# Input weights of the mixing block: split during retention and read back from DRAM, its convolution taps rearranged

## The chip, the cores and the metric

One core of one Trainium2 chip runs the whole program. The metric is the device time of one execution in microseconds (us), as the median over runs. Five engines work side by side, each through its own list of instructions in a fixed order: TensorE (PE, matmul; its weight loads are PEld), VectorE (DVE), ScalarE (ACT), GpSimd (POOL) and SyncE (SP, which here only issues DMAs). DMAs move data between DRAM and the on-chip memory (SBUF).

## The reference, cut to what matters

Two blocks of a network on 1024 tokens of width 1024. The first has four branches (a to d, sparse, banded, stick-breaking attention and retention), each gated and merged by products with the normalised input `h`; the second is the mixing block with an MLP behind it.

```python
def hybrid_layer(x, c, ...):
    h = rms_norm(x, norm_g) * (1.0 + scale) + shift
    ... = jnp.split(h @ w_in, IN_OFFSETS, axis=-1)
    for i, (y, z) in enumerate(branches):          # d, retention, comes first in the kernel
        yi = y.reshape(B, S, BRANCH_W) * jax.nn.silu(z)
        term = jax.nn.sigmoid(h @ w_merge[i]) * (yi @ w_br[i])
        merged = term if merged is None else merged + term
    return x + gate * (merged @ w_out)

def second_block(x, p, ...):
        z = rms_norm_2(h, g_mix_pre[i]) @ w_in[i]
        conf_ab, q, k, v, f_logit, sc_h, sc_b, sc_c, pool_v = jnp.split(z, SPLIT_IDX, axis=-1)
        y_conf = conformer_conv(conf_ab, ...)      # a * sigmoid(b), 31 taps per channel, norm, silu, product
        y_att = forgetting_attention(q, k, v, f_logit + b_forget[i])      # 4 heads, softmax
        y_sc = sc_b * causal_depthwise_conv(sc_c * sc_h, w_sc[i])         # 3 taps
        y_pool = multiscale_pool(pool_v, ...)
        mix = jnp.concatenate([y_conf, y_att, y_sc, y_pool], axis=-1) @ w_out[i]
```

Retention, with chunks of 128 tokens, n = 0 to 7: scores of the chunk with a decay mask, times v, plus `q` times a state `R` that is handed from chunk to chunk; then each head is normalised.

## The kernel before, in words

All float32 operands of the large products are split into two parts, hi (the value rounded by a copy) and lo (the rest), and a product is three matmuls, hi by hi, hi by lo, lo by hi (`mm3`, L229 to L231). A product of 512 columns over a depth of 1024 is 24 matmuls. Weights are loaded by `load_w` (L187 to L205) in slabs of 128x1024 (512 KB): a raw tile `wr` by a DMA on SP's queue (L194), a hi tile `wh` by `copy` (L147 on ScalarE, L149 on VectorE) and a lo tile `wl` by `sub_lo` (L155 on POOL, L157 on VectorE). All three come from one set of nine buffers, tag "w"; a slab can be loaded only when a buffer is free. Wider tiles (activations, accumulators) come from 31 "blk" buffers.

A scheduler reads the program in the order written, gives each instruction its place on its engine by priorities and its own estimate of the time, and so fixes the lists. `stream(name, priority)` ranks what is issued inside it.

**Branch d** (L665 to L755) runs retention. Per chunk: scores (L700) into PSUM tiles `s`, mask on VectorE (L702), the product with `R` (L711) and with v (L714) into `o`, the state's update (L724 on TensorE, L731 on VectorE), statistics and normalisation (L737 to L744), transposes (L276) back. Behind a chunk, `FD` (L25, used at L751) may put other work: 'g' is `pre` (L635 to L652), a group of four merge products `h @ w_merge` whose tanh (L647) is stored to DRAM by SP (L649); 'b' is the sum for the gate of the layer. Its value is {0: 'g', 1: 'b', 6: 'g'}. After the loop, `y.gate` makes the product with `z` and silu. PSUM tiles of such products are called `mm`.

**Mixing** (L1286 to L1600). Its input weights `w_in_2` are loaded and split by `load_w` group by group: conformer a and b (`conf_group`, two channel halves m), q and k of the first two heads (`qk_group`), v with the forget logits (`tok_group`), then short convolution, pooling, the second q and k. The conformer's 31 taps (`tap`, L1329 to L1334) are VectorE instructions over 512 columns: two channel halves m by two token halves, 124 in all. `conv_steps` (L242) hands them out in turn; the string `WORK` (L25, loop at L1610) sets what follows: 's0' and 's1' the short convolution, 'A' and 'B' tiles of the attention over the first and second two heads, 'p' pooling, 't' and 'u' the rest of the taps, 'c' the rest of the conformer. After each A tile CS=4 tap steps are handed out. `softmax_pair` (L828 to L866) scales the probabilities of two heads through `copy` (L150 on VectorE) on the engine that `NORM2` names. `k_tiles` makes hi and lo tiles of k, with the unused 64 rows of each lo tile cleared on POOL (L770); `scores` (L797, L799) multiplies.

## Time and profile before

| | us |
|---|---|
| median of 3 runs | 2337.06 |
| lowest and highest | 2331.92, 2338.48 |
| the profiled execution | 2339.66 |
| its span on the core | 2337.8 |

The profile is of one execution, at a mean granted TensorE clock of 0.988. Its times count from the span's start. Busy shares are PE 96%, DVE 65%, ACT 41%, POOL 21%. Retention runs from about 78 to 228 us, mixing from about 1195 to 1560. Matmuls overlap in the records: their ends are modelled, so the distance of two starts tells the rate, and the busy time somewhat more than that.

### The profile page before, as it was taken

The numbers are of one execution on the slowest core, as the hardware profiler recorded it, in microseconds if no ns is written. First come the engines' busy times: TensorE is split into PE (matmuls) and PEld (weight loads), VectorE is DVE, ScalarE is ACT, GpSimd is POOL, SyncE is SP. The second block draws the span as 40 slices with busy tenths as digits, with TensorE's granted clock in tenths as the row PEclk, the third lists the DMA queues.
The fourth block names the chain that finished last, engine by engine and source line by source line (L and its number), as shares of the span: only waits on it lengthen the run. The fifth ranks groups of instructions, "written<-read, shape, count | busy, mean of one in ns | idle before, by whom it ended". The sixth has DMA issues, their size and how long they took to land.

```text
span 2337.8 us, 30294 instructions
## 1 busy us (share of the span) xinstructions
PE 2239.1 (96%) x11004; PEld 1854.8 (79%) x11004; DVE 1519.8 (65%) x2952; ACT 963.0 (41%) x1937; POOL 491.1 (21%) x411
## 2 busy tenths in 40 slices
PE   8999999999988999999998998999999999999898
PEld 6788888888877778877887876777888878888787
DVE  7634456665677865634479777756666776677773
ACT  6211344444545544422322344534544453344442
POOL 4222100010265622234320000012143430000021
PEclk9999999999999999999999999999999999999999
DMA  9421221122132343224221210156556595534222
GB/s 326 156 92 62 59 68 55 46 86 68 41 102 79 109 132 94 83 80 153 90 73 36 64 59 28 56 179 205 169 182 191 194 360 193 173 108 157 94 75 90
DMA packets 202783, 272.72 MB, mean 117 GB/s; under 512 B 17086, under 2 KB 126214, under 8 KB 202634
## 3 DMA queue, kind: packets, MB, share of 16 engines
q1 hardware_dynamic: 194240, 257.95, 34.1%
q10 hardware_dynamic: 8394, 12.84, 1.7%
q8 instruction: 87, 1.43, 0.3%
q14 instruction: 62, 0.51, 0.1%
...
## 4 chain that ended last, share of the span: by engine, by line
PE 46%; DVE 6%; DMA 2%; ACT 1%; issue 1%; POOL 0%; SPq 0%; DVEq 0%; POOLq 0%; ACTq 0%
PE mm L230 6%; PE mm L231 6%; PE mm L229 6%; DVE blk L1334 2%; PE s L1674 2%; PE s L1676 2%; PE s L1675 2%; PE t L276 1%; PE t L2014 1%; PE t L2015 1%; PE t L2016 1%; PE s L2015 1%; PE mm L2015 1%; PE s L2016 1%; PE mm L2016 1%; PE t L1674 1%
## 5 line engine op out<-in xcount | busy, mean ns | idle before, releaser
L229 PE MATMUL mm<-blk,wh 128*128 128x512 f32 x1264 | 505.1, 400 | 16.3 <-DVE tz L1149 7.0
L230 PE MATMUL mm<-blk,wh 128*128 128x512 f32 x1264 | 501.1, 396 | 0.9 <-DVE blk L157 0.9
L231 PE MATMUL mm<-blk,wl 128*128 128x512 f32 x1264 | 499.9, 396 | 1.9 <-POOL wl L155 1.5
L229 PEld LDWEIGHTS mm<-blk,wh 128*128 128x128 f32 x1264 | 238.6, 189 | 68.5 <-DVE tz L1149 9.8
L231 PEld LDWEIGHTS mm<-blk,wl 128*128 128x128 f32 x1264 | 238.6, 189 | 52.0 <-POOL wl L155 1.9
L230 PEld LDWEIGHTS mm<-blk,wh 128*128 128x128 f32 x1264 | 238.7, 189 | 47.5 <-DVE blk L157 1.3
L155 POOL TENSOR_TENSOR wl<-wr,wh 128x1024 fp32r<-128x1024 f32 (+1 forms) x50 | 122.6, 2453 | 479.7 <-ACT wh L147 281.3
L229 PE MATMUL mm<-wh,blk 128*128 128x512 f32 (+3 forms) x544 | 197.3, 364 | 6.2 <-DVE wh L149 1.8
L231 PE MATMUL mm<-wh,blk 128*128 128x512 f32 (+3 forms) x544 | 194.9, 360 | 1.0 <-DVE blk L157 1.0
L157 DVE SCALAR_TENSOR_TENSOR wh<-blk,wh 128x1024 fp32r<-128x1024 f32 x116 | 138.5, 1222 | 72.0 <-issue 56.4
L147 ACT ACTIVATE wh<-blk 128x1024 fp32r<-128x1024 f32 x116 | 116.9, 1053 | 163.1 <-PE s L2015 77.2
L230 PE MATMUL mm<-wl,blk 128*128 128x512 f32 (+3 forms) x480 | 171.1, 357 | 9.5 <-DVE wl L157 9.1
L147 ACT ACTIVATE blk<-mm 64x512 fp32r<-64x512 f32 (+3 forms) x138 | 77.9, 570 | 172.6 <-PE mm L231 112.6
L147 ACT ACTIVATE PT<-t 128x512 fp32r<-128x512 f32 (+3 forms) x224 | 96.0, 460 | 117.4 <-PE o L816 65.0
L157 DVE SCALAR_TENSOR_TENSOR PT<-t,PT 128x512 fp32r<-128x512 f32 (+3 forms) x224 | 110.9, 515 | 38.0 <-ACT PT L147 37.2
L147 ACT ACTIVATE wh<-wr 128x1024 fp32r<-128x1024 f32 (+2 forms) x91 | 93.7, 1031 | 99.4 <-DMA wr<-in_w_in_dram 22.5
L309 POOL TENSOR_TENSOR sm<-sm,mhalf 128x1 f32<-128x1 f32 x64 | 38.0, 597 | 444.3 <-DVE sm L308 428.6
L229 PEld LDWEIGHTS mm<-wh,blk 128*128 128x128 f32 x544 | 104.1, 192 | 24.5 <-DVE wh L149 2.6
L231 PEld LDWEIGHTS mm<-wh,blk 128*128 128x128 f32 x544 | 104.1, 192 | 16.9 <-DVE blk L157 1.8
L230 PEld LDWEIGHTS mm<-wl,blk 128*128 128x128 f32 x480 | 92.3, 192 | 24.2 <-DVE wl L157 11.3
L157 DVE SCALAR_TENSOR_TENSOR wl<-wr,wh 128x1024 fp32r<-128x1024 f32 (+2 forms) x69 | 88.2, 1279 | 30.8 <-PE mm L230 14.0
L1150 POOL TENSOR_TENSOR acc<-tz,acc 128x512 f32<-128x512 f32 x48 | 68.8, 1436 | 132.0 <-DVE tz L1149 91.4
...
## 6 DMA issues: line engine op xcount, KB each, us to landing
...
```

The source lines that it names most:

```text
L147: return ac.activation(dst, src, AF.Copy, scale=1.0 if scale is None else scale)
L155: po.tensor_tensor(lo, x, hi.bitcast(F32), op=ALU.subtract)
L157: ve.scalar_tensor_tensor(out=lo, in0=x, scalar=scale, in1=hi.bitcast(F32), op0=ALU.mult, op1=ALU.subtract)
L229: pe.matmul(dst, sh, mh, start=(i == 0), stop=False)
L230: pe.matmul(dst, sh, ml, start=False, stop=False)
L231: last = pe.matmul(dst, sl, mh, start=False, stop=(i == n - 1))
L1150: po.tensor_tensor(acc[:], t[:], acc[:], op=ALU.add)
L1334: ve.scalar_tensor_tensor(out=acc[:, c:c1], in0=u[:, c - l:c1 - l], scalar=w, in1=acc[:, c:c1], op0=ALU.mult, op1=ALU.add)
L1674: pe.matmul(dst, wh, xh, start=first and k == 0, stop=False, skip_group_check=True)
L1675: pe.matmul(dst, wh, xl, start=False, stop=False, skip_group_check=True)
L2015: pe.matmul(d, sh[:, c, ts_], tl[:, c, :], start=False, stop=False)
L2016: last = pe.matmul(d, sl[:, c, ts_], th[:, c, :], start=False, stop=stop)
```

## The change

1. `w2_split` splits all of `w_in_2` in 20 steps: 16 slabs of 128x1024 and 4 of 128x520. A step loads the raw slab (SP, two DMAs where it holds two groups of columns), makes hi on ScalarE and lo on VectorE, and stores both to DRAM (SP). `FD` calls three steps behind each of the chunks 0 to 6 of retention.
2. In mixing `load_w2` reads hi and lo by DMAs on POOL's queue; no split is left there.
3. The taps: channel half m=0 takes taps 0 to 15 by token halves, 16 to 30 over whole rows of 1024; m=1 takes all 31 over whole rows. `conv_steps` ranks them behind by TAPL=1000, and finishes one series before the next. 't' in `WORK` now stands for all that is left of them, 'u' is gone.
4. One of the two scalings of `softmax_pair` in the mixing's attention is on ScalarE (`NORM2='av'`).
5. `k_tiles` keeps one lo tile for two heads; nothing is cleared, and the lo matmul contracts 64 rows.
6. `short_conv` multiplies by `sc_b` straight from PSUM, in two halves, without a copy of it. Two casts (`identR`, `causR`) are issued earlier.

```diff
-_T = dict(..., FD={0: 'g', 1: 'b', 6: 'g'}, ..., NORM='v', NORM2='v', CS=4, CSB=8, ..., WORK='s0 A A A A A A A A p s1 q t c B c B c B c B c 0a 1a P w 5 4 6 7 g 2 3a e u c B e c B c e B c c e B 1b 0b 3b', ...)
+_T = dict(..., FD={0: 'gw', 1: 'bw', 2: 'w', 3: 'w', 4: 'w', 5: 'w', 6: 'gw'}, ..., NORM='v', NORM2='av', TAPL=1000, CS=4, CSB=8, ..., WORK='s0 A A A A A A A A p s1 q t c B c B c B c B c 0a 1a P w 5 4 6 7 g 2 3a e c B e c B c e B c c e B 1b 0b 3b', ...)
...
     def conv_steps(n):
-        for _ in range(n):
-            if convs:
-                half, steps_ = convs.pop(0)
-                if next(steps_, "end") != "end":
-                    convs.insert(sum(h == half for h, _ in convs), (half, steps_))
+        with stream("taps", tc.tile_snap_priority() + _T["TAPL"]):
+            for _ in range(n):
+                if convs and next(convs[0], "end") == "end":
+                    convs.pop(0)
...
+    w2_cols, w2_d = {}, {}
+    for m in range(2):
+        w2_cols["conf", m] = ([m * P, 256 + m * P], P, 4)
+    w2_cols["qk", 0] = ([512, 768], P, 4)
+    w2_cols["v", 0] = ([1024], 260, 2)
+    w2_cols["qk", 1] = ([512 + P, 768 + P], P, 4)
+    for m in range(2):
+        w2_cols["sc", m] = ([1284 + m * P, 1796 + m * P], P, 4)
+        w2_cols["sb", m] = ([1540 + m * P], P, 8)
+    w2_cols["pool", 0] = ([2052], 256, 4)
+
+    def w2_split():
+        for key, (cs_, n, per) in w2_cols.items():
+            N = n * len(cs_)
+            for b in range(KC // per):
+                raw = main.tile([P, per, N], F32, name=nm("wr"), tag="w", bufs=NW)
+                for i, c0 in enumerate(cs_):
+                    sy.dma_start(raw[:, :, i * n:(i + 1) * n], w_in2[:, b * per:(b + 1) * per, c0:c0 + n])
+                hi, lo = [main.tile([P, per, N], F32R, name=nm("wh"), tag="w", bufs=NW) for _ in range(2)]
+                copy(hi[:], raw[:], "a")
+                sub_lo(lo[:], raw[:], hi[:])
+                for j, t in enumerate((hi, lo)):
+                    d = dram.tile([P, per, N], F32R, name=nm("w2"), tag=nm("w2"), bufs=1)
+                    sy.dma_start(d[:].bitcast(F32), t[:].bitcast(F32))
+                    w2_d[key, b, j] = d
+                yield
+
+    def w2_ahead():
+        for _ in range(3):
+            next(w2_steps, None)
+
+    def load_w2(*key):
...
+        for b in range(KC // per):
+            for j, p_ in enumerate((w.h, w.l)):
+                p_[b] = main.tile([P, per, n * len(cs_)], F32R, name=nm("wh"), tag="w", bufs=NW)
+                po.dma_start(p_[b][:], w2_d[key, b, j][:])
...
             for c in _T["FD"].get(n, ""):
-                dict(g=pre, p=lambda: proj(0), P=lambda: proj(1), a=ada_gate, b=ada_gate_sum)[c]()
+                dict(g=pre, w=w2_ahead, p=lambda: proj(0), P=lambda: proj(1), a=ada_gate, b=ada_gate_sum)[c]()
...
     def k_tiles():
-        kh, kl = [blk(F32R), blk(F32R)], [blk(F32R), blk(F32R)]
-        for hh in range(2):
-            po.memset(kl[hh][64 - hh * 64:128 - hh * 64, :].bitcast(F32), 0.0)
-        return kh, kl
+        kh, kl = [blk(F32R), blk(F32R)], blk(F32R)
+        return kh, [(kl, slice(hh * 64, hh * 64 + 64)) for hh in range(2)]
...
-            pe.matmul(b[:, :w], qs[:, qc], kl[:, ks], start=False, stop=not last)
+            kl_, r = kl if isinstance(kl, tuple) else (kl, slice(0, P))
+            pe.matmul(b[:, :w], qs[r, qc], kl_[r, ks], start=False, stop=not last)
...
-    def conv(m, half):
-        for l in range(31):
-            tap(accs[m], us[m], l, dwc[:, m, 30 - l:31 - l], l == 0, half * 512, half * 512 + 512)
+    def conv(m, ls, halves=((0, S),)):
+        for l in ls:
+            for c0, c1 in halves:
+                tap(accs[m], us[m], l, dwc[:, m, 30 - l:31 - l], l == 0, c0, c1)
             yield
...
         z_half(hT2, w, 0, evac)
-        convs.append((0, conv(m, 0)))
+        if m == 0:
+            convs.append(conv(0, range(16), ((0, 512),)))
...
         z_half(hT2, first[m], 1, conf_evac[m])
-        convs.append((1, conv(m, 1)))
+        if m == 0:
+            convs.append(conv(0, range(16), ((512, S),)))
+            convs.append(conv(0, range(16, 31)))
+        else:
+            convs.append(conv(1, range(31)))
...
-    tok_group(hT2, load_w([(w_in2[:, :, 1024:1284], 0)], 260, per=2), 256, 4, lambda t, b: vF.put(t, b, 1.0), fl)
+    tok_group(hT2, load_w2("v", 0), 256, 4, lambda t, b: vF.put(t, b, 1.0), fl)
```

The orders below are those of the engines' lists, without the rows' numbers.

TensorE in retention, before: here chunk 3 begins, `s` are scores (L700), `mm_1824` and `mm_1853` are the first two products of the second merge group ('g' behind chunk 6 in the program, run early), `t` transposes.

```order
L229 MATMUL mm_1853<-blk_432,wh_1816 128x512
L230 MATMUL mm_1853<-blk_433,wh_1816 128x512
L231 MATMUL mm_1853<-blk_432,wl_1817 128x512
L700 MATMUL s_1589<-blk_779,blk_781 128x128
L700 MATMUL s_1589<-blk_780,blk_782 128x128
L700 MATMUL s_1594<-blk_779,blk_781 128x128
L700 MATMUL s_1594<-blk_780,blk_782 128x128
L229 MATMUL mm_1853<-blk_432,wh_1816 128x512
L230 MATMUL mm_1853<-blk_433,wh_1816 128x512
L231 MATMUL mm_1853<-blk_432,wl_1817 128x512
L229 MATMUL mm_1853<-blk_511,wh_1816 128x512
L276 MATMUL t_1583<-c_63,Pm_1578 128x128
```

TensorE at the same place in the change, from the end of chunk 2 on:

```order
L770 MATMUL s_1623<-blk_1060,kz_1621 128x128
L770 MATMUL s_1627<-blk_1060,kz_1621 128x128
L746 MATMUL s_1685<-blk_779,blk_781 128x128
L746 MATMUL s_1685<-blk_780,blk_782 128x128
L746 MATMUL s_1690<-blk_779,blk_781 128x128
L746 MATMUL s_1690<-blk_780,blk_782 128x128
L275 MATMUL t_1649<-c_63,Pm_1644 128x128
L275 MATMUL t_1704<-c_63,blk_781 128x128
L275 MATMUL t_1704<-c_63,blk_782 128x128
L275 MATMUL t_1649<-c_63,Pm_1644 128x128
L757 MATMUL o_1684<-blk_1284,qx_1695 128x128
L760 MATMUL o_1684<-blk_1060,Pm_1688 128x64
```

Before, 24 matmuls of `mm_1824` stand between chunk 2's `kz` product and chunk 3's scores, and further products between each two pieces of chunks 3 to 7. In the change those chunks' 76 rows follow each other directly; the second merge group (`mm_2016` and on, with `wh_2008`) comes after chunk 7.

SP's queue, before, from the first merge group's weights on (`wr_1337`, `wr_1339`): the second group's (`wr_1812`, `wr_1814`) follow at once.

```order
L194 DMA wr_1337<-in_w_merge_dram 128x4x256
L194 DMA wr_1339<-in_w_merge_dram 128x4x256
L194 DMA wr_1812<-in_w_merge_dram 128x4x256
L194 DMA wr_1814<-in_w_merge_dram 128x4x256
L194 DMA wr_1983<-in_w_in_dram 128x8x128
L649 DMA pre_1376<-tz_1374 128x512
L649 DMA pre_1405<-tz_1403 128x512
L649 DMA pre_1434<-tz_1432 128x512
```

SP's queue in the change, at the last steps before the second merge group's weights (`wr_2004`, `wr_2006`). L672 loads a raw slab, L678 stores hi or lo (`wh` copied by ScalarE first, subtracted by VectorE second).

```order
L678 DMA w_446_1923<-wh_1919 128x1024
L672 DMA wr_1927<-in_w_in_dram 128x4x128 x2
L678 DMA w_448_1925<-wh_1920 128x1024
L678 DMA w_453_1934<-wh_1930 128x1024
L672 DMA wr_1938<-in_w_in_dram 128x8x128
L678 DMA w_455_1936<-wh_1931 128x1024
L678 DMA w_460_1944<-wh_1940 128x1024
L194 DMA wr_2004<-in_w_merge_dram 128x4x256
L194 DMA wr_2006<-in_w_merge_dram 128x4x256
L678 DMA w_462_1946<-wh_1941 128x1024
L672 DMA wr_2132<-in_w_in_dram 128x4x256
L678 DMA w_504_2138<-wh_2134 128x1024
```

The second group's loads moved behind 18 steps. A raw load stands behind the hi store of the step before it (`wr_1927` behind the store of `wh_1919`, `wr_1938` behind that of `wh_1930`), and so it is along the whole series.

VectorE in mixing, before, while v is made: taps (L1334) of both channel halves, `blk_11223` and `blk_11224`, around the evacuations of v (`mm_11898`) and the splits (`wl`).

```order
L1334 SCALAR_TENSOR_TENSOR blk_11223<-blk_11225,dwc,blk_11223 128x512
L1334 SCALAR_TENSOR_TENSOR blk_11224<-blk_11312,dwc,blk_11224 128x512
L157 SCALAR_TENSOR_TENSOR blk_11676<-mm_11898,blk_11676 128x4x64
L149 COPY fl<-mm_11898 128x4
L157 SCALAR_TENSOR_TENSOR wl_11968<-wr_11961,wh_11967 128x1024
L1334 SCALAR_TENSOR_TENSOR blk_11224<-blk_11312,dwc,blk_11224 128x482
L157 SCALAR_TENSOR_TENSOR wl_11972<-wr_11964,wh_11971 128x1024
L1334 SCALAR_TENSOR_TENSOR blk_11223<-blk_11225,dwc,blk_11223 128x512
L1334 SCALAR_TENSOR_TENSOR blk_11224<-blk_11312,dwc,blk_11224 128x512
L1380 TENSOR_TENSOR fl<-fl,bf 128x32
```

VectorE in the change, in the second tile of the attention: the taps of m=1 (`blk_11430`), over whole rows, between the pieces of the softmax (L871, L883) and of the short convolution (`blk_12257`).

```order
L1371 TENSOR_SCALAR blk_11430<-blk_11512,dwc 128x1024
L1374 SCALAR_TENSOR_TENSOR blk_12257<-blk_12134,dwc,blk_12257 128x1022
L871 TENSOR_REDUCE blk_12325<-o_12326 64x128
L1374 SCALAR_TENSOR_TENSOR blk_11430<-blk_11512,dwc,blk_11430 128x1023
L883 ISA Pm_12427,mx_12420<-s_12428,xb_12323 128x384
L883 ISA mx_12420 128x1
L883 ISA Pm_12474,mx_12473<-s_12475,xb_12321 128x512
L883 ISA mx_12473 128x1
L157 SCALAR_TENSOR_TENSOR PT_12396<-t_12393,PT_12396 128x2x128
L157 SCALAR_TENSOR_TENSOR PT_12404<-t_12401,PT_12404 128x2x128
```

The taps of m=1 moved from the stretch of conformer, q, k and v into the attention's first tiles, and are twice as wide.

## Rows read from the trace of the kernel before

**Rows 1.** Page: busy time by engine; chain that ended last, by engine.

```profile
PE 2239.1 (96%) x11004; PEld 1854.8 (79%) x11004; DVE 1519.8 (65%) x2952; ACT 963.0 (41%) x1937; POOL 491.1 (21%) x411
...
PE 46%; DVE 6%; DMA 2%; ACT 1%; issue 1%; POOL 0%; SPq 0%; DVEq 0%; POOLq 0%; ACTq 0%
```

**Rows 2.** Stretches: length, busy PE, PEld, DVE, ACT, POOL; clock, DMA share, GB/s.

```profile
167.00:241.00 74.00, 72.23 (x385) 59.02 (x385) 36.39 (x130) 14.24 (x29) 19.84 (x21) 1.00 0.23 70
241.00:340.00 99.00, 99.00 (x535) 83.10 (x534) 48.04 (x166) 42.42 (x111) 8.07 (x4) 1.00 0.19 57
1195.00:1300.00 105.00, 95.02 (x489) 80.78 (x488) 102.18 (x170) 22.76 (x39) 3.30 (x4) 0.93 0.16 42
1300.00:1410.00 110.00, 107.72 (x551) 90.18 (x550) 82.44 (x182) 41.78 (x89) 1.90 (x2) 1.00 0.19 56
1410.00:1530.00 120.00, 103.91 (x498) 79.84 (x497) 85.33 (x229) 60.86 (x134) 9.86 (x11) 0.96 0.15 49
1256.00:1266.00 10.00, 7.69 (x34) 7.39 (x35) 9.90 (x17) 1.36 (x3) 0.00 (x0) 0.51 0.19 52
```

**Rows 3.** The same view for instructions on mm tiles alone (PE first).

```profile
167.00:212.00 45.00, 36.66 (x145) 26.45 (x146) 2.05 (x3) 3.00 (x5) 1.00 0.22 71
167.00:225.00 58.00, 47.67 (x189) 34.30 (x189) 3.42 (x5) 4.19 (x7) 1.00 0.24 73
167.00:241.00 74.00, 61.58 (x247) 45.09 (x248) 5.37 (x8) 4.80 (x8) 1.00 0.23 70
167.00:260.00 93.00, 76.42 (x309) 56.68 (x310) 8.11 (x12) 8.36 (x14) 1.00 0.24 68
```

**Rows 4.** Groups by form, 130 to 253 (520-wide: 1195 to 1300).

```profile
L155 POOL TENSOR_TENSOR wl<-wr,wh 128x1024 fp32r<-128x1024 f32 x5 | 11.9, 2387 | 30.6 <-ACT wh L147 30.6
...
L147 ACT ACTIVATE wh<-wr 128x1024 fp32r<-128x1024 f32 x8 | 8.5, 1056 | 12.9 <-PE mm L230 5.4 <-DMA wr<-in_w_in_dram 3.8 <-DMA wr<-in_w_merge_dram 3.3
...
L157 DVE SCALAR_TENSOR_TENSOR wl<-wr,wh 128x1024 fp32r<-128x1024 f32 x5 | 6.1, 1219 | 3.7 <-POOL wl L155 3.4 <-PE mm L230 0.4
...
L147 ACT ACTIVATE wh<-wr 128x520 fp32r<-128x520 f32 x3 | 1.9, 632 | 0.0
```

**Rows 5.** Weight loads: issue (min/median/max ns) and landing in mixing; landing 125 to 235.

```profile
L194 SPq DMA_DIRECT2D wr<-in_w_in_dram x13: 367/368/510, 1210.4 to 1287.7; - x13
...
DMA to landing us min/median/max: 2.8/3.4/5.2
...
DMA to landing us min/median/max: 4.2/4.5/5.4
```

**Rows 6.** Timeline of SP, 136 to 138 us.

```profile
136.92 0.95 SPq L194 DMA_DIRECT2D wr<-in_w_merge_dram  x2
```

**Rows 7.** Timeline of ScalarE, 141 to 152 us.

```profile
147.65 0.60 ACT L647 ACTIVATE tz<-mm 128x512 f32<-128x512 f32 x1 [3.73 <-PE mm L231]
```

**Rows 8.** Timeline of TensorE, 167 to 174 us: start, length.

```profile
167.87 0.50 PE L229 MATMUL mm<-blk,wh 128*128 128x512 f32 x1 [0.85 <-DVE blk L551]
168.21 0.39 PE L230 MATMUL mm<-blk,wh 128*128 128x512 f32 x1
...
173.94 0.39 PE L231 MATMUL mm<-blk,wl 128*128 128x512 f32 x1
```

**Rows 9.** Forty slices of 85 to 120 us: DMA in GB/s.

```profile
GB/s 48 19 70 264 265 0 0 0 0 0 0 60 253 106 286 375 398 405 407 400 398 382 391 389 375 216 4 174 137 0 0 9 0 19 158 365 76 0 0 0
```

**Rows 10.** VectorE groups: 1195 to 1310 (two rows), 1300 to 1410, 1300 to 1530.

```profile
L1334 DVE SCALAR_TENSOR_TENSOR blk<-blk,dwc,blk 128x512 f32<-128x512 f32 (+24 forms) x120 | 82.4, 737 | 0.4
L157 DVE SCALAR_TENSOR_TENSOR wl<-wr,wh 128x1024 fp32r<-128x1024 f32 (+1 forms) x10 | 10.1, 1008 | 0.0
...
L1334 DVE SCALAR_TENSOR_TENSOR blk<-blk,dwc,blk 128x1023 f32<-128x1023 f32 x2 | 2.6, 1282 | 0.0
...
L150 DVE TENSOR_SCALAR Pm<-Pm,sm 128x128 f32<-128x128 f32 (+7 forms) x32 | 15.3, 514 | 0.4
```

**Rows 11.** Waits of TensorE, 1200 to 1300: total, times, longest.

```profile
PE mm L230 <- DVE wl L157: 4.4, 2, 2.9
```

More of the change, by code (lines that the diff above doesn't have):

```diff
@@ L652, in pre @@
         del pre_todo[:n]
+    w_in2 = kview(I["w_in_2"][0])
+    w2_cols, w2_d = {}, {}
[23 more added lines that the diff above has]
+                yield
+    w2_steps = w2_split()
+    def w2_ahead():
+        for _ in range(3):
+            next(w2_steps, None)
+    def load_w2(*key):
+        cs_, n, per = w2_cols[key]
+        w = W()
+        w.h, w.l = {}, {}
+        for b in range(KC // per):
+            for j, p_ in enumerate((w.h, w.l)):
+                p_[b] = main.tile([P, per, n * len(cs_)], F32R, name=nm("wh"), tag="w", bufs=NW)
+                po.dma_start(p_[b][:], w2_d[key, b, j][:])
+        w.hi = lambda k, c0, c1: w.h[k // per][:, k % per, c0:c1]
+        w.lo = lambda k, c0, c1: w.l[k // per][:, k % per, c0:c1]
+        return w
     def branch_d():
@@ L1284, in hybrid_then_mix_kernel @@
     out_phase(gT, [half_w(w_o, 0, False), half_w(w_o, 1, True)], evac_out1, finish_out1)
-    w_in2 = kview(I["w_in_2"][0])
     mix = A()
-    def wcols2(*c):
-        n = 256 // len(c)
-        return load_w([(w_in2[:, :, a:a + n], i * n) for i, a in enumerate(c)], 256)
     def conf_group(m):
-        u, w = blk(), wcols2(m * P, 256 + m * P)
+        u, w = blk(), load_w2("conf", m)
         def evac(b, j, half):
@@ L1363, in xb @@
         return cur[0].tile(list(shape), dt, name=nm("xb"), tag="xb", bufs=2)
+    identR = cur[0].tile([P, P], F32R, name="identR", tag="identR", bufs=1)
+    ve.tensor_copy(identR[:], ident)
+    causR = cur[0].tile([P, P], F32R, name="causR", tag="causR", bufs=1)
+    ve.tensor_copy(causR[:], C2["causal"])
     for m in range(2):
         z_half(hT2, first[m], 1, conf_evac[m])
-        convs.append((1, conv(m, 1)))
+        if m == 0:
[3 more added lines that the diff above has]
+            convs.append(conv(1, range(31)))
     qk0, w, evac = qk_group(0)
@@ L1492, in short_conv, with evac, times @@
     def short_conv(m):
-        if True:
-            hh_, u, bb = blk(), blk(), blk()
-            def evac(b, j, half):
-                cs = slice(half * 512, (half + 1) * 512)
-                if j == 0:
-                    copy(hh_[:, cs], b[:], "a")
-                else:
-                    ve.tensor_mul(u[:, cs], b[:], hh_[:, cs])
-            z_group(hT2, wcols2(1284 + m * P, 1796 + m * P), evac)
-            z_group(hT2, load_w([(w_in2[:, :, 1540 + m * P:1540 + (m + 1) * P], 0)], 128),
-                    lambda b, j, half: copy(bb[:, half * 512:(half + 1) * 512], b[:], "a"), ms=(0,))
-            for l in range(3):
-                tap(hh_, u, l, dwc[:, m, 33 - l:34 - l], l == 0)
-            ve.tensor_mul(hh_[:], hh_[:], bb[:])
-            y32[4 + m] = hh_
+        u, held = blk(), {}
+        def evac(b, j, half):
+            if j == 0:
+                held[half] = tmp("tz", 512)
+                copy(held[half][:], b[:], "a")
+            else:
+                ve.tensor_mul(u[:, half * 512:(half + 1) * 512], b[:], held[half][:])
+        z_group(hT2, load_w2("sc", m), evac)
+        y = y32[4 + m] = blk()
+        for l in range(3):
+            tap(y, u, l, dwc[:, m, 33 - l:34 - l], l == 0)
+        def times(b, j, half):
+            cs = slice(half * 512, (half + 1) * 512)
+            ve.tensor_mul(y[:, cs], b[:], y[:, cs])
+        z_group(hT2, load_w2("sb", m), times, ms=(0,))
     def pooling():
@@ L1516, in pooling @@
         gs = [blk(), blk()]
-        z_group(hT2, wcols2(2052), lambda b, m, half: copy(gs[m][:, half * 512:(half + 1) * 512], b[:], "a"))
+        z_group(hT2, load_w2("pool", 0), lambda b, m, half: copy(gs[m][:, half * 512:(half + 1) * 512], b[:], "a"))
         for m in range(2):
@@ L1577, in out_early, with conv_rest @@
             yield
-    def conv_rest(half):
-        while any(h <= half for h, _ in convs):
+    def conv_rest():
+        while convs:
             conv_steps(1)
     steps = dict(A=attention(0), B=attention(1), c=conf_rest(), e=out_early())
-    works = dict(g=load_gains, s0=lambda: short_conv(0), s1=lambda: short_conv(1), t=lambda: conv_rest(0), u=lambda: conv_rest(1), P=lambda: pool_out(), q=second_qk, p=pooling)
+    works = dict(g=load_gains, s0=lambda: short_conv(0), s1=lambda: short_conv(1), t=conv_rest, P=lambda: pool_out(), q=second_qk, p=pooling)
     for c in steps:
```

10 lines of the change are left out of this document (3 added, 7 removed).

## Prediction

> **What bounds the kernel now.** I read the page first: TensorE is busy 96% of the span and leads the chain of waits with 46%, VectorE comes second with 65% and 6% [rows 1]. So a change pays where TensorE waits for VectorE, and costs where TensorE is left without work. Then I read busy time in stretches, for the two places that the edit touches [rows 2]. Mixing, 1195 to 1300 us: VectorE is busy 102.18 of 105 us, TensorE only 95.02, at a mean granted clock of 0.93; VectorE sets the pace there. From 1300 to 1410 TensorE is busy 107.72 of 110, VectorE 82.44. From 1410 to 1530 both have gaps. Retention, 167 to 241 us: TensorE is busy 72.23 of 74 us, VectorE 36.39, ScalarE 14.24. It looks as if two engines had room there. What the share doesn't show is why TensorE is full: the products on the mm tiles (merge products, gates and the next branch's first ones, no part of the retention chain) make 61.58 us of it, 247 matmuls [rows 3]; the retention steps themselves need little. That filler is the point of this prediction.
>
> **The change, retention side.** Twenty split steps are hung into chunks 0 to 6. Each takes three of the nine "w" buffers, loads a slab, copies hi on ScalarE, forms lo on VectorE, and stores both. On the engines that is cheap: 16 copies of 1.06 and 4 of 0.63 us on ScalarE, 16 subtractions of 1.22 and 4 of some half of that on VectorE [rows 4], so 19.5 and 22 us, in stretches with more room than that. I cost it at nothing by itself.
>
> The SP queue is another matter. It runs in order, and in the new order the load of step i+1 stands behind the store of step i's hi, which waits for ScalarE's copy, which waits for the load of step i. So the steps are a chain, one at a time. Its period, for slabs of two halves: store and two issues at 0.37 each, of which the last starts 0.74 us after the store, landing 3.4 [rows 5], copy 1.06, together 5.3 with 0.1 for the hand-over; for one-piece slabs 0.37 + 4.5 + 1.06 = 5.9; for the four 260-column slabs 0.37 + 3.4 + 0.63 = 4.4. The landings are medians of loads of this kind, 4.5 in 125 to 235 us, 3.4 in mixing, where most are halves.
>
> Start: the first w2 load takes the place of the third merge load, at 136.9 us [rows 6]. Landing 4.5, copy 1.06: 142.5. Step 2: 147.8. Step 3's second half sits behind a store of tanh that ends at 148.25 [rows 7] and behind lo of step 2 (147.8 + 1.22), so about 149.5 + 3.4 + 1.06 = 154.
>
> Who waits for that: the second group of four merge products. Before, its weights were loaded at 136.9, and its products began at 167.87 [rows 6, 8]; y.gate's products followed. Now its two loads stand behind the hi store of step 18 and its buffers are those of steps before. Steps 4 to 18 are 9 of halves, 2 in one piece, 4 small: 47.7 + 11.8 + 17.6 = 77 us, to 231. Two issues, landing and copy add 6.3; with POOL's lo still to come (2.39 [rows 4]) I take **241 us** for TensorE's restart. Until then its order holds chunks 3 to 7 of retention and nothing else.
>
> Price: at 241 the old kernel had done the same retention and 247 product matmuls more. Their slot is 0.229 us: 26 starts from 168.21 to 173.94 [rows 8]. 247 x 0.229 = **56.6 us late**, and nothing behind catches up, since 241 to 340 is full too (99.00 of 99) [rows 2]. Bounds: no faster than the data moves, 1.57 MB a step (0.52 in, 1.05 out) at the 400 GB/s that the best slices show [rows 9], so 3.9 us and 2.0 for small ones: restart at 154 + 51 + 6.6 = 212, 145 matmuls [rows 3], 33 us. No slower than every landing at the worst 5.2 [rows 5]: 27 us later, 268, some 336 matmuls by the row to 260, 77 us. I stay by the medians.
>
> Then the clock: from 1256 to 1266, after the wait of 2.9 us for a lo, TensorE was granted 0.51, the 1.2 GHz level [rows 2, 11]; 10 us at half rate lose 5. The restart may pay the same or nothing: I take 2.
>
> **The change, mixing side.** VectorE loses, in 1195 to 1300: half the taps (m=1's 60 of 120 at 0.737, 44 us), and nearly all of 10 lo subtractions (10.1) [rows 10]. 102 falls to about 50, TensorE becomes the bound. To win: its idle 105 - 95.02 = 10, and the half-clock stretches, 2 x 0.07 x 105 = 15 us at half rate, worth 7. I leave 2 for hand-overs: 15.
>
> In 1300 to 1410 the 31 whole-row taps of m=1 arrive: 30 x 1.28 and a cheaper first, 39 us by duration, and some 37 by starts, as each overlaps the next a little [rows 10]; the ones that ran there before (about 6 us) and a quarter of the scalings (15.3 / 4) go. 82.4 + 37 - 6 - 3.8 = 109.6 of 110: VectorE just full, as TensorE is. I put 0, with -5 to +10. In 1410 to 1530 a quarter of the scalings leaves VectorE (3.8), but a 1024-wide one on ScalarE takes about the 1.06 of its copies against 0.745, and stands before the next tile's work: 0, -5 to +4. The four memsets of half a tile on POOL, the lo matmul that contracts 64 rows (columns set its slot), four ScalarE copies and the short convolution's products in halves are covered: nothing, and 1 us if the cover is gone.
>
> The w2 tiles now come over POOL's queue, which carries no DMA before; the nearest price is SP's 3.4 to 4.5 us. They are issued as the "w" buffers come free, ahead of use, so I cost them at nothing. A rule speaks against that: the Trainium skill, SBUF — State Buffer, section "Who interferes with whom", says that descriptors of a GpSimd-queue DMA are written by GpSimd, which is locked out while VectorE runs a copy, cast or scaling in its two-port mode. No run here shows it so far. It is weighed among the rivals.
>
> **Sum**, against the profiled execution, 2339.66 (span 2337.8): + 56.6 + 2 - 15 = 2383.3. That execution is 2.6 above the median of the runs, so **2381**.
>
> **Rivals.**
> - *The chain goes at the speed of the data.* Restart at 212, 33 us late: 2357. For it: the 70 GB/s of that stretch are little [rows 2]. Against: each load waits for a copy, so nothing overlaps but the stores. 0.16.
> - *Weights late in mixing.* Each of ten groups could wait for its tiles as the longest wait for a lo does now, 2.9 us [rows 11]. From five groups on the 15 us are eaten: 2396; at ten 29 us are lost: 2410. For it: eight tiles of v fill the buffers, so qk1 and sc0 load at the last moment, and POOL's queue also holds row sums and norms behind these issues. Against: mixing's VectorE work is nearly all taps, which read two tiles. By the skill's rule these taps would not lock GpSimd out, the 32 scalings would. 0.12.
> - *Every landing is slow*, as a load, two stores and the next load share the queues: 77 us, 2401. 0.06.
> - *Not slower.* Mixing gives back more than retention costs. TensorE's idle time from 1195 to 1530 is 10 + 2.3 + 16.1, and half clock costs 7 + 5 there (0.93 and 0.96): 40 us is the ceiling. It decides only if the restart comes by some 222 us, where the row to 225 has 189 matmuls, 43 us. With the chain at its fastest: 2339.7 + 33 + 2 - 40 - 2.6 = 2332. Against: in attention VectorE is fuller than before. 0.04.
>
> **The numbers.** My case has 0.62; it runs from 2367 to 2395 by a period 1 us off either way and by mixing's bounds. The range 2350 to 2404 takes in the fast chain, the slow one and the lighter half of late weights; it leaves out the last rival and the heavy end. A measurement of this kernel can tell some 0.3% (7 us) from no change: faster, under 2330, needs more than the last rival's price, 0.03; within, 0.03; slower 0.94.
>
> **What would show it.** TensorE: a stretch from about 167 to 241 us with only retention's lines busy, ended by the merge weights (wh, wl) of the second group. SP: w2 loads 4 to 6 us apart from 137 to about 245, each after a hi store. Everything after that some 55 us late, so that mixing starts near 1250. In mixing, TensorE above 97% in its first 90 us and VectorE down to half; in the attention's first heads VectorE near 95%. I am wrong if products stand among chunks 3 to 7, if the steps overlap, or if mixing gains 40.

## The result and the profile after

The change takes 2429.66 us (median of 4 runs, 2425.59 to 2433.97) beside 2334.78 for the kernel before on the same chip: a ratio of 1.0403, with a 95% interval of 1.0381 to 1.0424. That is 49 us over the forecast and 26 over its upper end. The profiled execution took 2425.59 us, its span is 2423.9, 86.1 more than before.

On the page the share of TensorE hardly moves, from 96% to 95% [rows 1]. One group has a new wait of 35.4 us for ScalarE's `wh`, and the list of queues has a new one, POOL's (software_dynamic):

```profile
PE 2291.7 (95%) x11004; PEld 1880.2 (78%) x11004; DVE 1510.9 (62%) x2889; ACT 978.5 (40%) x1954; POOL 500.4 (21%) x441
...
q0 software_dynamic: 5760, 18.91, 2.4%
...
PE 45%; issue 3%; DMA 2%; DVE 2%; ACT 1%; POOL 1%; ACTq 0%; POOLq 0%; DVEq 0%; SPq 0%
...
L229 PE MATMUL mm<-blk,wh 128*128 128x512 f32 x1264 | 507.1, 401 | 43.5 <-ACT wh L147 35.4
```

TensorE is busy 52.6 us more in all, with the same 11004 matmuls: busy time that grows at an equal count points to matmuls that run slower, as well as to a wait. The stretches of the change (columns as in [rows 2]):

```profile
167.00:241.00 74.00, 33.15 (x151) 29.17 (x149) 37.11 (x125) 13.22 (x24) 11.46 (x16) 0.55 0.74 232
241.00:257.00 16.00, 0.08 (x1) 0.08 (x1) 2.45 (x2) 3.17 (x3) 0.06 (x1) 0.50 0.76 239
257.00:263.00 6.00, 5.62 (x13) 4.00 (x14) 2.56 (x2) 2.11 (x2) 2.31 (x1) 0.53 0.55 210
263.00:340.00 77.00, 77.00 (x384) 63.02 (x384) 19.59 (x31) 21.64 (x34) 13.25 (x8) 1.00 0.40 114
1265.00:1370.00 105.00, 102.41 (x542) 87.12 (x543) 66.80 (x102) 19.15 (x38) 12.54 (x23) 0.98 0.27 87
1370.00:1500.00 130.00, 123.38 (x563) 96.25 (x562) 100.10 (x192) 41.86 (x91) 6.36 (x11) 0.93 0.23 75
1430.00:1460.00 30.00, 23.38 (x86) 16.09 (x86) 28.07 (x54) 10.96 (x22) 0.53 (x1) 0.72 0.17 54
```

Where [rows 2] had 385 matmuls and 72.23 busy us in 167 to 241, the change has 151 in 33.15, at a granted clock of 0.55, nearly down to the 1.2 GHz level. From 241 to 257 TensorE only starts one matmul, at the very end. From 263 on it is full, so nothing is caught up. Mixing starts at about 1265: its first 105 us are what was hoped for (TensorE 102.41 busy, VectorE 66.80), the stretch behind has gaps again, and in 1430 to 1460 VectorE is nearly full (28.07 of 30) with TensorE at 23.38 and a clock of 0.72.

A ledger says where the 86.1 us arise: how much later than before the same instruction starts.

| instruction | late by, us | added since the row above | forecast |
|---|---|---|---|
| branch a's first scores | 75.8 | 75.8 | 56.6 + 2 |
| branch b's first softmax (branch c lies between) | 80.9 | 5.1 | 0 |
| last products of out1 | 79.6 | -1.3 | 0 |
| conformer's first | 83.6 | 4.0 | (2 for hand-overs, within the -15) |
| forget gates' scan | 63.5 | -20.1 | -15 |
| last tile of attention A | 89.2 | 25.7 | 0 (-5 to 10) |
| end of the span | 86.1 | -3.1 | 0 |

Two rows carry the miss: retention, 17 us dearer than forecast, and attention A, 26.

The place of the wait. Timeline of SP, 208 to 226 us (start, length):

```profile
209.19 0.34 SPq L678 DMA_DIRECT2D w<-wh  x1
209.59 1.39 SPq L672 DMA_DIRECT2D wr<-in_w_in_dram  x2
211.07 4.84 SPq L678 DMA_DIRECT2D w<-wh  x2
215.97 1.70 SPq L672 DMA_DIRECT2D wr<-in_w_in_dram  x2
217.76 6.19 SPq L678 DMA_DIRECT2D w<-wh  x2
224.04 0.39 SPq L672 DMA_DIRECT2D wr<-in_w_in_dram  x1
```

Each load (L672) follows at once on a store (L678) that has stood waiting. The loads' landing in the view of their line, and what ScalarE waited for from 135 to 262 us (total, times, longest):

```profile
DMA to landing us min/median/max: 3.4/4.4/6.0
```

```profile
ACT wh L147 <- DMA wr<-in_w_in_dram: 84.6, 18, 6.6
```

18 times, up to 6.6 us, ScalarE stands without work until a raw slab lands: the chain of one step at a time, as forecast. But from step 4 on the steps of 512 KB are 6.4 to 7.0 us apart, two of them 7.4 and 8.1, not 5.3 to 5.9; only v's small ones, 4.4 to 5.0, are near their 4.4. The second merge group's loads, and TensorE's timeline at the end of the wait:

```profile
251.00 1.37 SPq L194 DMA_DIRECT2D wr<-in_w_merge_dram  x2
```

```profile
256.92 0.80 PE L229 MATMUL mm<-blk,wh 128*128 128x512 f32 x1 [35.42 <-ACT wh L147]
```

And the first instruction of branch a's compression, before and after, in the view of its line:

```profile
L988 PE MATMUL t<-blk,blk x64: 222/223/243, 249.0 to 252.7; 128*64 128x32 f32 x64
```

```profile
L1033 PE MATMUL t<-blk,blk x64: 222/223/243, 325.6 to 329.3; 128*64 128x32 f32 x64
```

### The profile page after: what moved, and what is told of

The parts are those of the page before. It is cut to its first block, busy times and chain, and to the rows that moved or that the text cites. A ratio compares the mean times of both kernels' runs of the same rounds, so it can differ in the third digit from the quotient of the medians.

```text
span 2423.9 us, 30385 instructions
## 1 busy us (share of the span) xinstructions
PE 2291.7 (95%) x11004; PEld 1880.2 (78%) x11004; DVE 1510.9 (62%) x2889; ACT 978.5 (40%) x1954; POOL 500.4 (21%) x441
## 4 chain that ended last, share of the span: by engine, by line
PE 45%; issue 3%; DMA 2%; DVE 2%; ACT 1%; POOL 1%; ACTq 0%; POOLq 0%; DVEq 0%; SPq 0%
PE mm L229 6%; PE mm L230 6%; PE mm L231 6%; PE s L1723 2%; PE s L1722 2%; PE s L1724 2%; PE t L275 2%; PE t L2062 1%; PE t L2064 1%; PE t L2063 1%; PE t L1723 1%; PE mm L2063 1%; PE t L1722 1%; PE t L1724 1%; PE mm L2064 1%
## 5 line engine op out<-in xcount | busy, mean ns | idle before, releaser
L229 PE MATMUL mm<-blk,wh 128*128 128x512 f32 x1264 | 507.1, 401 | 43.5 <-ACT wh L147 35.4
L230 PE MATMUL mm<-blk,wh 128*128 128x512 f32 x1264 | 501.7, 397 | 0.9 <-DVE blk L157 0.9
L231 PE MATMUL mm<-blk,wl 128*128 128x512 f32 x1008 | 399.1, 396 | 1.7 <-POOL wl L155 1.7
L155 POOL TENSOR_TENSOR wl<-wr,wh 128x1024 fp32r<-128x1024 f32 (+1 forms) x48 | 116.7, 2432 | 536.9 <-ACT wh L147 346.2
L231 PEld LDWEIGHTS mm<-blk,wl 128*128 128x128 f32 x1008 | 190.4, 189 | 43.3 <-POOL wl L155 2.9
L230 PE MATMUL mm<-wl,blk 128*128 128x512 f32 (+2 forms) x416 | 151.4, 364 | 4.0 <-DVE wl L157 4.0
L229 PEld LDWEIGHTS mm<-wh,blk 128*128 128x128 f32 x544 | 102.9, 189 | 20.1 <-ACT blk L147 2.4
L275 PE MATMUL t<-c,Pm 128*128 128x128 f32 x508 | 87.8, 293 | 21.9 <-DVE Pm L790 12.2
L231 PE MATMUL mm<-blk,wh 128*128 128x512 f32 x256 | 101.5, 397 | 0.1
L1195 POOL TENSOR_TENSOR acc<-tz,acc 128x512 f32<-128x512 f32 x48 | 68.5, 1429 | 127.9 <-DVE tz L1194 88.6
```

The costliest lines, as they stand in the source:

```text
L155: po.tensor_tensor(lo, x, hi.bitcast(F32), op=ALU.subtract)
L229: pe.matmul(dst, sh, mh, start=(i == 0), stop=False)
L230: pe.matmul(dst, sh, ml, start=False, stop=False)
L231: last = pe.matmul(dst, sl, mh, start=False, stop=(i == n - 1))
L275: pe.transpose(dst, src, ident)
L1195: po.tensor_tensor(acc[:], t[:], acc[:], op=ALU.add)
```

## The experiments

Each ratio is to the kernel before on the same chip, with its 95% interval. "Lateness" is the ledger's, against the profile of before.

**1. The two halves apart.** `mix_only` keeps the mixing side of the change and splits in mixing as before; `split_only` adds the early split alone to the kernel before.

```diff
-FD={0: 'gw', 1: 'bw', 2: 'w', 3: 'w', 4: 'w', 5: 'w', 6: 'gw'}
+FD={0: 'g', 1: 'b', 6: 'g'}
...
 def load_w2(*key):
     cs_, n, per = w2_cols[key]
-    w = W()
...
+    return load_w([(w_in2[:, :, c0:c0 + n], i * n) for i, c0 in enumerate(cs_)], n * len(cs_), per=per)
```

> No split step during retention: FD as before, and mixing loads and splits its weights as before, on SP, ScalarE, VectorE and POOL; the taps, the scaling, the lo tile and the short convolution stay as changed. Theory 1 (the split steps keep TensorE without products in retention, 76 us): products of retention as before, first product of the second merge group near 168 us, time 2335 plus what mixing alone does. Mixing: with the splits still on VectorE its first 105 us win less than the 12 of the change, about 4; the attention over the first two heads still loses some 17: 2340 to 2355. Rival (the loss comes from elsewhere, say from the lo tile in the branches or from mixing): stays above 2390.

> The kernel before with only the early split: 20 steps behind chunks 0 to 6, read back over POOL's queue; taps, scaling, lo tile and short convolution as before. Theory 1: retention is late by 76 us as in the change, with TensorE restarting near 257. Mixing wins what the splits held up there, VectorE less 12 of 102 us, so 5 to 12, less 3 for the slower start: 2400 to 2408. Rival (what mixing loses, it loses to the weights that come over POOL's queue and not to the taps): as slow as the change, 2425 to 2430.

Measured: `mix_only` 2345.19 us, 1.0039 (1.0025 to 1.0053); `split_only` 2408.68, 1.0312 (1.0296 to 1.0327). `mix_only` lies in its first theory's window, `split_only` 0.7 us over its own. The split costs most of the loss. The mixing side, forecast to gain 15, loses by itself: it is 15.4 us early at the scan and 6.7 late at the last tile of attention A.

**2. Which wait ends the chain.** `group_first` puts the second merge group ahead of the first split step, so that its products are TensorE's filler again. `loads_pool` moves the raw loads to POOL's queue, where no store stands ahead of them.

```diff
-FD={0: 'gw', 1: 'bw', 2: 'w', 3: 'w', 4: 'w', 5: 'w', 6: 'gw'}
+FD={0: 'ggw', 1: 'bw', 2: 'w', 3: 'w', 4: 'w', 5: 'w', 6: 'w'}
```

```diff
-                    sy.dma_start(raw[:, :, i * n:(i + 1) * n], w_in2[...])
+                    po.dma_start(raw[:, :, i * n:(i + 1) * n], w_in2[...])
```

> The change, with the second group of four merge products ahead of the first split step (FD 0 is 'ggw', 6 is 'w'). Theory 1a (the end of the chain of steps is what TensorE waits for): the four products, 96 matmuls of 0.229 us, run early, but the next weights, y.gate's, stand behind the last two steps, so TensorE restarts near 272 instead of 257: only 5 to 10 won, 2420 to 2425. Rival 1b (only the amount of products at hand counts): 22 won, 2408.

> The change, with the raw loads of the split steps on POOL's queue, the stores still on SP: a load no longer stands behind the store of the step before. Theory 1c (the serial order on SP sets the period of 6.4 to 7 us): loads run ahead by the nine buffers, the period falls to 4.5 to 5.5, TensorE restarts near 225 to 235, time 2400 to 2410. Rival 1d (the DMA engines set it: they are busy for 0.74 of that stretch, at 232 GB/s): the period stays above 6, restart after 248, time 2420 to 2430.

`group_first`: 2437.35 us, 1.0426 (1.0409 to 1.0444), slower than the change; both theories missed. TensorE runs through the group's products early and then waits for y.gate's weights, which now stand behind all 20 steps:

```profile
290.94 0.79 PE L229 MATMUL mm<-blk,wh 128*128 128x512 f32 x1 [43.09 <-ACT wh L147]
```

So putting these products first only moved the wait: whatever weights are loaded on SP behind the steps come late, and here, with all 20 steps ahead of them, later still. `loads_pool`: 2414.19, 1.0332 (1.0317 to 1.0348), between the two theories. Its restart, and the stretch ahead of it (columns as in [rows 2]):

```profile
237.35 0.79 PE L229 MATMUL mm<-blk,wh 128*128 128x512 f32 x1 [26.89 <-ACT wh L147]
```

```profile
190.00:230.00 40.00, 13.21 (x52) 11.22 (x52) 19.69 (x55) 10.31 (x15) 14.73 (x19) 0.50 0.91 308
```

Taking the raw loads out of SP's order is worth 20 us of the restart. The order isn't all gone, though: the second merge group's own loads are still on SP, behind the hi store of step 18.

```profile
228.99 0.32 SPq L678 DMA_DIRECT2D w<-wh  x1
229.53 1.65 SPq L194 DMA_DIRECT2D wr<-in_w_merge_dram  x2
```

And the DMA engines are now busy 0.91 of the time, at 308 GB/s in the mean. From 190 to 230 us, in slices of 1 us:

```profile
GB/s 246 150 308 17 174 341 338 199 29 283 250 393 418 229 270 236 307 413 417 315 180 303 258 188 279 393 389 279 328 385 406 401 385 402 393 381 393 406 430 414
```

The last 11 slices are at 381 to 430: the 400 GB/s that my fastest case took from [rows 9] are reached, with loads and stores mixed, but only late in the series.

**3. The stores' bytes.** `small_stores` keeps SP's order and every wait, and stores a part of each slab; mixing splits as before.

```diff
-                    sy.dma_start(d[:].bitcast(F32), t[:].bitcast(F32))
+                    sy.dma_start(d[:, 0:1].bitcast(F32), t[:, 0:1].bitcast(F32))
```

> The change with its 20 split steps in their places, but each store writes only a part of its slab (a quarter of most, a half of v's, an eighth of two), and the mixing loads and splits its input weights for itself as before. The order of SP's queue in retention stays as in the change. If the steps were slower than I forecast because the loads land late among their own stores' traffic: the loads land in a median of 3.3 to 3.7 us instead of 4.4, TensorE restarts at 235 to 244 us, and the kernel takes 2396 to 2406 us (mix_only's 2345 and some 55 late). If the period lies in issuing and reading and the stores' bytes don't matter: landing 4.2 to 4.5, restart at 250 to 257, 2408 to 2418 us.

Measured: 2407.66 us, 1.0312 (1.0284 to 1.034). Landings, SP's timeline and TensorE's restart:

```profile
DMA to landing us min/median/max: 3.2/3.7/4.3
```

```profile
206.61 1.06 SPq L672 DMA_DIRECT2D wr<-in_w_in_dram  x2
207.77 4.49 SPq L678 DMA_DIRECT2D w<-wh  x2
212.32 1.04 SPq L672 DMA_DIRECT2D wr<-in_w_in_dram  x2
```

```profile
246.21 0.80 PE L229 MATMUL mm<-blk,wh 128*128 128x512 f32 x1 [6.66 <-ACT wh L147]
```

The landing fits the first theory; its windows for restart and time are missed by 2 us (the time lies just under the second theory's), since the first load was issued at 139.49 us here and at 135.79 in the change. From that load to the merge group's loads pass 101.3 us (240.79), in the change 115.2 (251.00): the stores' bytes are 13.9 us of the chain. The forecast had 94 from the first load to the merge group's (136.9 to 231), so some 7 us are left that the stores' bytes don't explain. A pair of issues also took 1.0 us, not 1.39. 5.7 us from load to load is within my forecast's period.

**4. Fewer steps, or steps elsewhere.** `six_steps` leaves one step behind each of the chunks 0 to 5, the other slabs are split in mixing. `spread_a` hangs the 20 steps behind the tiles of branch a's attention, `spread_split` does so with the kernel before.

```diff
 def w2_ahead():
-    for _ in range(3):
-        next(w2_steps, None)
+    next(w2_steps, None)
...
```

```diff
-FA={(0, 2): 'g', (0, 3): 'mmm', (0, 7): 'qm', (1, 0): 'gg', (1, 6): 'gz'}
+FA={(0, 0): 'w', (0, 1): 'w', (0, 2): 'gw', (0, 3): 'mmmw', (0, 4): 'ww', ..., (1, 7): 'w'}
...
```

> The change, with one split step behind each of chunks 0 to 5 instead of three, six in all (conformer and first q, k); the other groups are loaded and split in mixing as before. Theory 1 (the loss is the chain ahead of the second merge group's weights, step by step): after step 3 at 157 us three more of 6.5, so those weights are loaded near 177 and TensorE goes on at 183 to 185: 57 to 61 matmuls of 0.229 late, 13 to 14 us instead of 76; with the rest of the change as in mix_only, 2355 to 2360. Rival (a fixed cost of having any steps among the chunks, by the halved clock or the engines' order): 2375 or more.

> The change, with the 20 split steps moved out of retention: one or two behind each tile of branch a's attention (340 to 640 us before, TensorE busy 100 of each 100 us, VectorE 60, ScalarE 45, DMA share 0.2). Theory 1: there the next weights of TensorE are far between, so no product waits for a step; the 76 us are gone, and what is left of the change is its mixing: 2335 + 5 + 3, so 2338 to 2350. Rival (the steps cost wherever they stand, by VectorE's and ScalarE's 22 and 20 us or by the DMA traffic): 2360 or more.

> The kernel before with only the early split, its steps behind the tiles of branch a's attention; taps, scaling, lo tile and short convolution as before. Theory 1, and theory 2 (mixing's loss in the change is that of its attention, by taps and scaling): the splits' 12 us of VectorE in mixing's first 105 us are won, at most 10 of them as time: 2325 to 2332, faster than both. Rival (weights over POOL's queue are late, or the start of mixing pays for them): 2335 to 2345.

`six_steps`: 2368.68 us, 1.0141 (1.0126 to 1.0156). The restart came 2 us after its window (186.68), but branch a starts 17.3 late, not 13 to 14, and the time lies between the two theories' windows. The clock is low around the restart:

```profile
167.00:185.00 18.00, 13.25 (x55) 10.63 (x56) 12.05 (x44) 2.44 (x4) 3.98 (x6) 0.63 0.89 278
185.00:205.00 20.00, 19.12 (x93) 15.91 (x94) 10.95 (x37) 4.66 (x8) 7.83 (x7) 0.82 0.43 135
```

`spread_a`: 2371.98, 1.0147 (1.0121 to 1.0173); `spread_split`: 2355.7, 1.0085 (1.0064 to 1.0106). Theory 1 missed in both; `spread_a` lies in its rival's window, `spread_split` beyond its rival's. Branch a's scores are at most 9 us late on the way and 4 to 5 early at the last tile, but by branch c's first scan both are 25 to 27 late. In `spread_split`:

```profile
540.00:560.00 20.00, 14.59 (x76) 10.95 (x77) 12.37 (x40) 8.81 (x20) 0.00 (x0) 0.94 0.86 277
560.00:580.00 20.00, 18.76 (x84) 14.95 (x83) 18.12 (x57) 13.01 (x28) 2.40 (x1) 0.72 0.70 213
```

The DMA share is 0.86 again and TensorE short of work: from 550.39 to 571.40 it starts no product on an mm tile. The weights of the next ones stand behind the steps on SP's queue there too (SP's timeline, then TensorE's):

```profile
564.88 1.34 SPq L194 DMA_DIRECT2D wr<-in_w_merge_dram  x2
571.40 0.51 PE L229 MATMUL mm<-blk,wh 128*128 128x512 f32 x1
```

How many steps SP's queue can carry unnoticed at one place wasn't found.

**5. The mixing parts.** `lo_128` gives the change back its lo tiles of k with 128 rows; `taps_old` its taps as before; `norm_v` both scalings on VectorE.

```diff
-        kh, kl = [blk(F32R), blk(F32R)], blk(F32R)
-        return kh, [(kl, slice(hh * 64, hh * 64 + 64)) for hh in range(2)]
+        kh, kl = [blk(F32R), blk(F32R)], [blk(F32R), blk(F32R)]
+        for hh in range(2):
+            po.memset(kl[hh][64 - hh * 64:128 - hh * 64, :].bitcast(F32), 0.0)
+        return kh, kl
...
-            pe.matmul(b[:, :w], qs[r, qc], kl_[r, ks], start=False, stop=not last)
+            pe.matmul(b[:, :w], qs[:, qc], kl[:, ks], start=False, stop=not last)
```

```diff
-    def conv(m, ls, halves=((0, S),)):
-        for l in ls:
-            for c0, c1 in halves:
-                tap(accs[m], us[m], l, dwc[:, m, 30 - l:31 - l], l == 0, c0, c1)
+    def conv(m, half):
+        for l in range(31):
+            tap(accs[m], us[m], l, dwc[:, m, 30 - l:31 - l], l == 0, half * 512, half * 512 + 512)
...
```

```diff
-NORM2='av'
+NORM2='v'
```

> The change, with the lo tiles of k as before: two tiles of 128 rows, the unused half cleared on POOL, the lo matmul over 128 rows. Theory 3 (a lo matmul over 64 rows between matmuls over 128 costs TensorE: in branch c, without early split, starts of a 512-wide lo stand 426 ns before the next instead of 231, and those of the hi ahead of it 367 instead of 236; 7.7 us in that branch's scores, 7.7 and 8.8 in the two halves of mixing's attention): branch c wins 4 to 5, mixing 10 to 16, so 2410 to 2416. Rival 2 (the taps in whole rows and VectorE make the attention slow; matmuls wait there anyway): only branch c's 4 to 5, 2425.

> The change, with the taps as before: all by token halves, handed out in turn over four series, not ranked behind. Theory 2a (whole-row taps of the second channel half among the attention's first tiles make VectorE the bound there, 17 us): the attention's tiles from 1370 on go at the pace of before, 17 won, of which the first stretch gives back 8 to 12, as it has the taps again: 2420 to 2425. Rival 2b (the scaling on ScalarE makes the attention slow): no gain, 2430 to 2440.

> The change, with both scalings on VectorE as before (NORM2 'v'). Theory 2b (the scaling on ScalarE stands in order before exponentials and copies, and a tile waits for it: the longest wait of TensorE there, 4.3 us, is for a Pm of ScalarE): 4 to 12 won, 2418 to 2426. Rival 2a (VectorE is the bound there by the taps): 4 us more work on VectorE, 2430 to 2434.

| kernel | us | ratio (95%) |
|---|---|---|
| `lo_128` | 2414.02 | 1.0335 (1.0319 to 1.035) |
| `taps_old` | 2420.38 | 1.0363 (1.0343 to 1.0384) |
| `norm_v` | 2431.98 | 1.0415 (1.0389 to 1.0441) |

`lo_128` and `taps_old` lie in their first theories' windows, `norm_v` in its rival's: the old taps win 9 us, the scaling on VectorE nothing.

The lo tile costs 15.6 us, and not by more work on VectorE: the rows show it in the distance of starts. Timeline of TensorE at a scores tile of 512 columns, before and after:

```profile
1345.14 0.39 PE L797 MATMUL s<-blk,blk 128*128 128x512 f32 x1
1345.37 0.40 PE L799 MATMUL s<-blk,blk 128*128 128x512 f32 x1
1345.60 0.63 PE L816 MATMUL o<-PT,blk 128*128 128x256 f32 x4
```

```profile
1411.00 0.45 PE L841 MATMUL s<-blk,blk 128*128 128x512 f32 x1
1411.38 0.50 PE L844 MATMUL s<-blk,blk 64*128 64x512 f32 x1
1411.81 0.98 PE L861 MATMUL o<-PT,blk 128*128 128x256 f32 x6
```

Before, each of the two holds TensorE for 0.23 us. After, the hi matmul (itself unchanged) holds it 0.38 us and the lo one, over half the rows, 0.43. The columns are the same: what has changed is that a matmul over 64 rows stands between two over 128. The Trainium skill, TensorEngine Tiling (Array Packing), section "Key Properties", says that a change of tiling mode, unlike a change of tile, drains TensorE; these rows agree, with 0.15 us ahead of the lo matmul and 0.20 behind it. Branch c shares `k_tiles`: `lo_128` has no loss there (77.7 us late at its first scan, 77.4 at branch b's first softmax), the change 5.1.

**6. The mixing side mended.** `mix_lo_128` is `mix_only` with `lo_128`'s edit; `mix_lo_128_taps_old` has `taps_old`'s too, and so keeps of the change the scaling on ScalarE, the short convolution from PSUM and the earlier casts.

> No split during retention, as in mix_only, and the lo tiles of k as before; the taps, the scaling and the short convolution stay as changed. Theory 3: 2345 less 14 to 20, so 2325 to 2331, faster than the kernel before. Rival 2: 2340.

> As mix_lo_128, with the taps as before too: what is left of the change is the scaling on ScalarE, the short convolution and the earlier casts. Theory 3 (then the taps are worth what the first stretch of mixing wins by them, less the tail in the attention): 2333 to 2338, that is 5 to 10 slower than mix_lo_128. Rival 2 (the taps cost): 8 faster than mix_lo_128.

`mix_lo_128`: 2330.58 us, 0.9979 (0.9969 to 0.999). `mix_lo_128_taps_old`: 2329.05, 0.9968 (0.9956 to 0.998), 4 us under its window. Both are faster than the kernel before, by 0.2% and 0.3%, just clear of the noise. Between them the taps are worth nothing. What the whole-row taps do is seen in the first stretch of each and the stretch behind it (`mix_lo_128` first):

```profile
1184.00:1292.00 108.00, 105.52 (x567) 90.54 (x566) 75.60 (x116) 27.91 (x52) 3.78 (x5) 1.00 0.19 55
1292.00:1340.00 48.00, 42.12 (x204) 35.21 (x202) 47.04 (x94) 17.52 (x44) 0.00 (x0) 0.88 0.12 34
```

```profile
1175.00:1295.00 120.00, 110.70 (x561) 93.68 (x561) 109.82 (x187) 26.52 (x48) 5.21 (x7) 0.94 0.16 45
1295.00:1340.00 45.00, 45.00 (x228) 37.86 (x227) 30.98 (x76) 17.62 (x43) 0.00 (x0) 1.00 0.20 60
```

With the new taps VectorE is relieved first and full behind (47.04 of 48), with the old ones the other way round. Of the 21 us that `mix_lo_128` has won by the scan, 3 are left at the first tile of attention B.

How much later each kernel has become since the scan, from the ledgers, at the last tile of attention A and, behind the rest of the taps, at the first tile of attention B:

| kernel | lo tile | taps | last of A, us | first of B, us |
|---|---|---|---|---|
| the change | 64 rows | new | 25.7 | 26.0 |
| `lo_128` | 128 rows | new | 10.9 | 21.7 |
| `taps_old` | 64 rows | old | 16.1 | 7.7 |
| `mix_only` | 64 rows | new | 22.1 | 22.4 |
| `mix_lo_128` | 128 rows | new | 5.8 | 18.0 |
| `mix_lo_128_taps_old` | 128 rows | old | -0.1 | 0.1 |

At the last tile of A it looks as if the lo tile were 15 to 16 of the 25.7 and the taps 6 to 10. At the first tile of B the taps are 18 (26.0 against 7.7, 18.0 against 0.1) and the lo tile 4: what the cheaper lo tile saves in A is lost again before B, while the rest of the taps is done. Some 4 come with the early split beside the new parts; `split_only`, with the old ones, loses nothing here (-0.5 and 0.3).

## Why the prediction was wrong

**What held.** The direction, and the mechanism that carried it: the steps are a chain through SP's queue, the second merge group's weights stand at its end, and TensorE has only chunks 3 to 7 until then. The first stretch of mixing gained 20.1 us, 16 after the 4.0 of the hand-over into it, where 15 was forecast, TensorE above 97% and VectorE at 64%. That nothing is caught up behind retention held too (77.00 busy of 77).

**The first failed term: the period, "store and two issues at 0.37 each, landing 3.4, copy 1.06, together 5.3".** The landing came from loads with few stores beside them [rows 5]. In the chain, the loads land among their own stores: a median of 4.4, the issue of a pair takes 1.39, most steps of 512 KB are 6.4 to 7.0 us apart, and the merge group's loads are issued at 251.0, not 231; the restart came at 256.9, not 241. That it missed by 16 and not by 20 is luck: the 241 held time for POOL's lo (2.39), which the first products, hi by hi, don't wait for. `small_stores` shows the cause of most of it: without most of the stores' bytes 3.7, 1.0 and 5.7. I had the slow case among the rivals, at 0.06, with 268 for the restart; the truth lies between the two. The price of a late restart, products listed by then at 0.229 us, held roughly. By the prediction's counting, this row of the kernel before (view of the mm tiles, as [rows 3]) gives 299 x 0.229 = 68.5:

```profile
167.00:257.00 90.00, 73.80 (x299) 54.83 (x300) 7.66 (x12) 7.76 (x13) 1.00 0.25 70
```

Measured: 75.8. The clock is part of the difference: it stays at half until about 262.5 us, so 5.6 us at half rate lose 2.8, where I took 2 for the whole. And by 257 the old kernel had also done the 64 matmuls of branch a's compression (249.0 to 252.7, the line of L988 above), 3.7 us that a count of mm tiles leaves out. That makes 75.0; 0.8 us stay unassigned.

**The second: the lo matmul over 64 rows, "columns set its slot", at nothing.** It was the one edit with work on TensorE that I waved through, and the trace of before had a row to price it by: retention's scores (L700) are over 64 rows, among products over 128.

```profile
174.26 0.72 PE L700 MATMUL s<-blk,blk 64*128 64x128 f32 x8
174.91 0.51 PE L229 MATMUL mm<-blk,wh 128*128 128x512 f32 x1
```

The product ahead of them, the last line of [rows 8], starts 0.32 us before them, not 0.229, while a transpose over 128 rows starts 0.23 behind its product (175.72 and 175.95): a change of rows was dear there too. The lo tile cost 15.6 us in the change and 14.6 without the early split, partly in branch c, which the prediction didn't name at all.

**The third: attention A at 0, from a VectorE "just full, as TensorE is".** The two engines, both full by their sums, did not both run full: in 1430 to 1460 VectorE is busy 28.07 of 30 and TensorE 23.38 (from 1370 to 1500 VectorE is at 77%, not near 95%). The term's upper bound was 10; without the lo tile, `lo_128` has lost 21.7 by the first tile of B, and with the old taps `mix_lo_128_taps_old` 0.1. The gain of the first stretch had been a loan: the work was moved behind, not taken away.

**Small ones.** The hand-over into mixing, part of my 2 us, cost 4.0. TensorE's timeline shows it waiting for the conformer's taps, loaded while POOL's queue fetches the first w2 tiles:

```profile
1264.99 0.43 PE L275 MATMUL t<-c,blk 31*128 31x31 f32 x4 [1.54 <-DMA blk<-in_w_conf_dw_dram]
```

It is in every run that fetches w2 tiles at the start of mixing (4 to 5.5 us) and not in `small_stores` (0.1) or `mix_only` (0), which don't; that the fetching causes it is argued from this, not tried alone. The scaling on ScalarE was put at -5 to +4 and is at most a small gain, within the noise: `norm_v` is 2 us slower than the change.

**The rivals.** *The chain at the speed of the data* fell: the restart came at 257, not 212. With only the raw loads off SP's queue, `loads_pool` restarts at 237; a chain free of every order wasn't run. *Weights late in mixing* fell as well. TensorE's waits from 1262 to 1530 us have this row for it (total, times, longest):

```profile
PE mm L230 <- DMA wh<-w: 0.7, 1, 0.7
```

The tiles landed in a median of 4.4 us, as SP's loads did, though one took 10.9. The Trainium skill's rule behind that rival (SBUF — State Buffer, section "Who interferes with whom") thus left no wait that counts here. *Every landing is slow* was nearest, for retention alone. *Not slower* was far: its 40 us ceiling met 84 us of lateness at the start of mixing.
